# A hybrid encoder layer: block copies on GpSimd, chunk tiles in another place, stores from ScalarE's queue

## Chip, core and metric

The kernel runs on one core of a Trainium2 chip. What is measured is the device time of one execution, in microseconds (us). A core has five engines that run their own instruction streams and wait for each other by semaphores: TensorE (PE in the profile, with its weight loads as PEld), VectorE (DVE), ScalarE (ACT), GpSimd (POOL) and SyncE (SP), which here does nothing but issue DMAs. Each engine takes its instructions in order: one that waits holds all that stand behind it. DMAs are issued from an engine's queue too and then run by themselves on 16 DMA engines.

## What is computed

One layer of an encoder over 1024 tokens of width 1024, in float32: a mixer, then cross-attention into 256 memory tokens, then a SwiGLU feed-forward part. The change touches the mixer and the keys and values of the memory. The mixer has two branches, from one input projection: windowed softmax attention, and a bidirectional gated DeltaNet, whose chunks of 64 tokens each need a triangular solve and then a scan over chunks. Cut to that:

```python
def _gated_delta_chunked(q, k, v, g, beta):
    ...
    lower = jnp.where(strict, jnp.einsum('bhnid,bhnjd->bhnij', kb, k) * decay, 0.0)
    tmat = lower + jnp.eye(c, dtype=jnp.float32)
    rhs = jnp.concatenate([v * beta[..., None], kb * jnp.exp(g)[..., None]], axis=-1)
    sol = lax.linalg.triangular_solve(tmat, rhs, left_side=True, lower=True, unit_diagonal=True)
    ...
    def step(state, inp):
        qg_i, kg_i, u_i, w_i, qk_i, gl_i = inp
        v_new = u_i - jnp.einsum('bhck,bhkv->bhcv', w_i, state)
        o_i = jnp.einsum('bhck,bhkv->bhcv', qg_i, state) + jnp.einsum('bhij,bhjv->bhiv', qk_i, v_new)
        state = state * gl_i[..., None, None] + jnp.einsum('bhck,bhcv->bhkv', kg_i, v_new)
        return state, o_i
```

## The kernel before

Products that need full float32 are made of two halves: a tile is split into a high part (whi, ph, s: a cast on ScalarE, L103) and the rest (wlo, pl: a difference on VectorE, or on GpSimd where the call says so, L104), and three products take the place of one. Weights come through load_w (L119), whose loads of raw weights into wraw are issued by SyncE at L126. The scheduler of the framework puts the instructions of each engine in an order of its own from the program's order and its dependences; the orders below are what is written.

Stage 1 (ORDER_1) makes the projection of the DeltaNet's heads, the convolution, norms and decays. It ends with base_inverse (L520) for each group g of two heads: the inverses of 32x32 diagonal blocks, row by row on VectorE (L544 to L546), for all blocks at once; the last two products are V on VectorE (L548) and A on GpSimd (L549), and both are stored to d_inv in DRAM (L553). Keys turned for the scan are stored to d_kv from the tile kt (L488).

Stage 2 (ORDER_2) is a list of work: A are the attention's projections (stored to d_q and d_k), V its values, G the gates (gate_proj, L777: a Silu on ScalarE into the tile gt, L782, then a store to d_gate, L783), L the levels of a head, W two windows of attention. levels(h) (L556) builds the full inverse out of the 32x32 blocks: it loads the blocks of its head from d_inv four times (cz, cw; L564), gathers them by ten copies of a quarter or half of the partitions (m5 and c6 on ScalarE, c5 on VectorE; L573 to L577), and goes through two levels of products: pair (L598) multiplies (L603), copies the result to bs on ScalarE (L605) and multiplies again (L609); between the levels stand z5 (L614) and mov6 (L616 to L623) and behind them Z (L625, L626), stored to d_pz. window(n, g) (L632) loads its queries into qr (L643), casts them to qs on ScalarE (L645), takes the rest on GpSimd (L646), makes the scores (L654), the softmax, and the product with the values (L680, L685).

Stage 3 (ORDER_3) is the scan. M is memory_norm (L917; its transposes are at L934), s01 is one step of both groups' scans (scan, L795), W windows still open, K a block of the memory's keys (next_keys, L941: weights in_w_ckv, products pck at L949, a copy to cv on ScalarE, L951, and a store, L952) and V of its values (next_values, L954: products pcv at L965, a copy to vv, L969, and a store, L970). A step loads a chunk of d_kv and d_pz for both directions (kv and pz; L824, L825) and makes its products (L809), with copies on ScalarE (vn, L846) and VectorE. Behind the scan come the output projection and the rest of the layer.

Tiles lie in pools, and a pool that is opened where another one lay waits for the last use of what it covers. The pool tl (L743, closed with p1) holds the tiles of the levels. The pool t3 (L793), opened on the right after p1 is closed, holds the scan's tiles: those of odd steps' chunks in both groups' pz and group 0's kv, and all of group 1's kv. Even steps' pz, and group 0's even kv, lie in the pool ra. All 28 stores from the tiles kt, gt, cv and vv are issued by SyncE.

Of the kernel before, what the change touches and what calls it, by code (L numbers as in the profile page):

```python
# [10 lines left out]
F32 = mybir.dt.float32  # L11
# [8 lines left out]
P = 128  # L20
# [4 lines left out]
HALF = 512  # L25
# [9 lines left out]


ORDER_1 = ("k0 k1 E0 K0 U0 E1 K1 U1 S0 q0 v0 q1 C0 v1 E2 C1 k2 E3 k3 q2 K2 U2 v2 K3 U3 S1 q3 C2 v3 C3 B0 B1").split()
ORDER_2 = "L0 L1 A4 V A0 A1 G0 G1 L2 L3 W W W A2 A3 G2 G3 W".split()
ORDER_3 = ("M " + "s01 W K " * 5 + "s01 K " * 3 + "s01 V V").split()


# [35 lines left out]
def tile_hybrid_block(  # L77
# [6 lines left out]
    nc = tc.nc  # L84
# [396 lines left out]
    def turned_keys(h):  # L481
        g, hh = h // 2, h % 2
        for b in range(2):
            c4 = slice(4 * b, 4 * b + 4)
            pk = turned(kqv["k", h], b)
            kt = t2.tile([P, 4, P], F32, tag="kt", name="kt")
            nc.scalar.copy(kt, pk)
            nc.sync.dma_start(d_kv[g][c4, :, hh, 0].rearrange("c p n -> p c n"), kt)  # L488
            ss = squares(pk, False)
            nc.gpsimd.tensor_scalar(xk[:, h, c4], ss, EPS, None, ALU.add)  # L490
            nc.gpsimd.tensor_tensor(rootk[:, h, c4], xk[:, h, c4], phalf[:, 0:4], ALU.pow)
# [64 lines left out]
    def levels(h):  # L556

        g, hh = h // 2, h % 2

        def blocks(name):  # L560
            return tl_.tile([P, NT, 32], F32, tag=name, name=name, bufs=1)

        def fetch(dst, i, d):
            nc.sync.dma_start(dst, d_inv[g][i][d, hh].rearrange("c b r s -> (b r) c s"))  # L564

        cz = [blocks("cz0"), blocks("cz1")]
        cw = [blocks("cw0"), blocks("cw1")]
        m5, c5, c6 = blocks("m5"), blocks("c5"), blocks("c6")
        for d in range(2):
            fetch(cz[d], 1, d)  # L570
            fetch(cw[d], 0, d)
        for q in range(4):
            r = slice(32 * q, 32 * q + 32)  # L573
            nc.scalar.copy(m5[r], cz[1 - q % 2][r])
            nc.vector.tensor_copy(c5[r], cw[q % 2][r])
        for d in range(2):
            nc.scalar.copy(c6[64 * d:64 * d + 64], cw[d][64 * d:64 * d + 64])  # L577
        def part(b):
            c4 = slice(4 * b, 4 * b + 4)

            def wide(name):
                return tl_.tile([P, 4, P], F32, tag=name, name=name, bufs=2)

            L5, L6, D5, D6 = wide("L5"), wide("L6"), wide("D5"), wide("D6")
            Z = [wide("Z0"), wide("Z1")]
            for e, dst, src in ((nc.vector, D5, c5), (nc.vector, D6, c6), (nc.vector, Z[0], cz[0]), (nc.vector, Z[1], cz[1])):
                e.tensor_tensor(dst.rearrange("p c (q n) -> p c q n", q=4), bc(src[:, c4, :], 2, (P, 4, 4, 32)),
                                        bc(dmask, 1, (P, 4, 4, 32)), ALU.mult)
            Ul = wide("Ul")
            nc.sync.dma_start(Ul, d_u[g][hh, c4].rearrange("c p n -> p c n"))  # L590
            yield
            p_ = small().rearrange("p (c n) -> p c n", c=4)
            for j in range(4):
                nc.tensor.transpose(p_[:, j, :], Ul[:, j, :], ident)
            nc.vector.tensor_tensor(L5, p_, bc(cm["m5"], 1, (P, 4, P)), ALU.mult)
            nc.vector.tensor_tensor(L6, p_, bc(cm["m6"], 1, (P, 4, P)), ALU.mult)

            def pair(lt, mv, dd, w):  # L598

                yield  # L600
                p_ = small()[:, 0:4 * w].rearrange("p (c n) -> p c n", c=4)
                for c in range(4):
                    nc.tensor.matmul(p_[:, c, :], lt[:, c, :], mv[:, c, :], start=True, stop=True)  # L603
                bs = tl_.tile([P, 4, 64], F32, tag="bs", name="bs", bufs=2)[:, :, 0:w]
                nc.scalar.copy(bs, p_)  # L605
                yield
                p_ = small()[:, 0:4 * w].rearrange("p (c n) -> p c n", c=4)
                for c in range(4):
                    nc.tensor.matmul(p_[:, c, :], dd[:, c, :], bs[:, c, :], start=True, stop=True)  # L609
                return p_  # L610

            p_ = yield from pair(L5, m5[:, c4, :], D5, 32)
            z5 = tl_.tile([P, 4, 32], F32, tag="z5", name="z5", bufs=2)
            nc.scalar.mul(z5, p_, -1.0)  # L614
            nc.vector.transpose(D6[32:64, :, 0:32], z5[0:32])
            nc.vector.transpose(D6[64:96, :, 96:128], z5[96:128])  # L616
            nc.vector.tensor_copy(Z[1][32:64, :, 0:32], z5[32:64])
            nc.vector.tensor_copy(Z[0][64:96, :, 96:128], z5[64:96])
            mov6 = tl_.tile([P, 4, 64], F32, tag="mov6", name="mov6", bufs=2)
            nc.scalar.copy(mov6[0:64], Z[1][0:64, :, 0:64])  # L620
            nc.vector.tensor_copy(mov6[64:128], Z[0][64:128, :, 64:128])
            nc.scalar.copy(Z[0][0:32, :, 32:64], z5[0:32])
            nc.scalar.copy(Z[1][96:128, :, 64:96], z5[96:128])  # L623
            p_ = yield from pair(L6, mov6, D6, 64)
            nc.scalar.mul(Z[0][0:64, :, 64:128], p_[0:64], -1.0)  # L625
            nc.vector.tensor_scalar(Z[1][64:128, :, 0:64], p_[64:128], -1.0, None, ALU.mult)  # L626
            for d in range(2):
                nc.sync.dma_start(d_pz[g][d][c4, :, hh, 1].rearrange("c p n -> p c n"), Z[d])

        together([part(b) for b in range(2)])  # L630
# [109 lines left out]
    tw = p12.enter_context(pool("tw", 2))  # L740
    tw.tile([P, 384], F32, tag="sc", name="sc", bufs=8)
    vhl = tw.tile([P, NT + 1, 2, 2, 64], F32R, tag="vhl", name="vhl", bufs=1)[:, 0:NT]
    tl_ = p1.enter_context(pool("tl", 2))  # L743

    def pair():
        t = ra.tile([P, 2, HALF], F32, tag="rr", name="rr", bufs=2)
# [30 lines left out]
    def gate_proj(h):  # L777

        pp = proj(w_in[:, 2304 + h * P:2304 + (h + 1) * P])
        for hf in range(2):  # L780
            gt = trp.tile([P, HALF], F32, tag="rop", name="gt")
            nc.scalar.activation(gt, pp[hf], AF.Silu)  # L782
            nc.sync.dma_start(d_gate[h * P:(h + 1) * P, hf * HALF:(hf + 1) * HALF], gt)  # L783

    issue(ORDER_2, {"A": attn_proj, "V": value_proj, "G": gate_proj, "L": levels, "W": next_windows})
    dump("d_q", d_q); dump("d_k", d_k); dump("d_gate", d_gate)
    p1.close()
    pgs.close()
# [6 lines left out]
    def scan(g):  # L795
# [16 lines left out]
        for step in range(NT):  # L812
# [1 line left out]
            cs = (step, NT - 1 - step)  # L814

            near = step % 2 == 0
            pz = (ra.tile([P, 2, 2, 2, P], F32, tag="rr", name="pz", bufs=2) if near else tl("pz", [P, 2, 2, 2, P], bufs=1))
            if g == 0:
                kv = (ra.tile([P, 2, 2, 4, P], F32, tag="sct", name="kv") if near else tl("kv", [P, 2, 2, 4, P], bufs=1))
            else:  # L820
                kv = tl("kv", [P, 2, 2, 4, P])
            before = loaded
            for d in range(2):
                loaded = nc.sync.dma_start(kv[:, d], d_kv[g][cs[d]])  # L824
# [116 lines left out]
    def next_keys():  # L941

        ct = kv_done[0]
        kv_done[0] += 1
        whi, wlo = load_w(w_ckv[:, ct * P:(ct + 1) * P], KT, P, nc.gpsimd)
        pp = pc.tile([P, 512], F32, tag="pc", name="pck")[:, 0:ML]
        for k in range(KT):
            for i, (w, a) in enumerate(((whi, 0), (whi, 1), (wlo, 0))):
                nc.tensor.matmul(pp, w[:, k, :], mT[a][:, k, :], start=(k == 0 and i == 0), stop=(k == KT - 1 and i == 2))  # L949
        cv = mk.tile([P, 512], F32, tag="cv", name="cv", bufs=2)[:, 0:ML]  # L950
        nc.scalar.copy(cv, pp)  # L951
        nc.sync.dma_start(d_mk[ct * P:(ct + 1) * P, :], cv)  # L952

    def next_values():  # L954

        ch = kv_done[1]
        kv_done[1] += 1
        pp = [pc.tile([P, 512], F32, tag="pc", name="pcv") for _ in range(2)]
        for kp in range(4):
            whi, wlo = load_w(w_ckv[kp * 256:(kp + 1) * 256, D + ch * 512:D + (ch + 1) * 512], 2, 512)  # L960
            for t in range(2):
                for kk in range(2):
                    k = 2 * kp + kk
                    for i, (w, a) in enumerate(((whi, 0), (whi, 1), (wlo, 0))):
                        nc.tensor.matmul(pp[t], mT[a][:, k, t * P:(t + 1) * P], w[:, kk, :], start=(k == 0 and i == 0),  # L965
                                         stop=(k == KT - 1 and i == 2))
        for t in range(2):
            vv = mk.tile([P, 512], F32, tag="cv", name="vv", bufs=2)
            nc.scalar.copy(vv, pp[t])  # L969
            nc.sync.dma_start(d_mv[t, :, ch * 512:(ch + 1) * 512], vv)  # L970

    scans = [scan(g) for g in range(2)]

# [264 lines left out]
    for e in range(EARLY):  # L1238
        f = 2 * e
# [320 lines left out]
```

## Time and profile before

| what | value |
|---|---|
| time, median of 3 runs | 1537.51 us |
| lowest and highest run | 1535.87 and 1537.88 us |
| span of the profiled execution | 1537.6 us |
| busy share of PE, VectorE, ScalarE, GpSimd | 96%, 69%, 48%, 24% |

The profiled execution's own time is its span, from the first to the last instruction. In the profile a line such as `L574 ACT COPY m<-cz 32x256 ... x16 | 6.5, 404 | 8.8 <-DMA` is a group of like instructions: line of the program, engine, operation, tile written and tile read, shape, count, then busy us in all and mean ns of one, then the engine's idle us just before them and what ended it. A line of a timeline begins with the start in us from the span's start and the duration. SPq is SyncE's queue of DMA issues; a DMA's duration there is the time of its issue, and its landing comes later. A line of waits gives the engine and line that waited, what for, the us in all, how many times, and the longest. The granted clock is the share of TensorE's full speed that the chip granted in a stretch.

### The profile page before, as it was taken

What the parts mean: (1) busy time and instruction counts of PE and PEld (TensorE: products, weight loads), DVE (VectorE), ACT (ScalarE), POOL (GpSimd) and SP (SyncE); (2) the same over time, 40 slices, a digit from 0 to 9 for tenths busy, and PEclk for the clock granted to TensorE, in tenths of its full rate; (3) what the DMA queues carried; (4) which work ended last, traced back from release to release, by engine and by line L of the source; (5) the groups of instructions that cost most, each with busy time, mean ns of one, the idle gap of its engine ahead of it and who ended that gap; (6) DMA issues with size and microseconds to landing.
All of it is one profiled execution on the core that took longest, in us unless ns stands there. A gap on an engine that the chain in (4) does not pass through costs nothing. (4 is left out here: it accounts for less than half of the span.)

```text
span 1537.6 us, 21036 instructions
## 1 busy us (share of the span) xinstructions
PE 1481.4 (96%) x7451; PEld 1246.6 (81%) x7451; DVE 1067.1 (69%) x1732; ACT 743.3 (48%) x1518; POOL 374.6 (24%) x364
## 2 busy tenths in 40 slices
PE   6999999998999899999999999999999999999997
PEld 5888888787999777888888877888888888888786
DVE  6868999686788776534346387776877555696665
ACT  6578732457457665454336564323223333354532
POOL 2020210111247103253102232443433432000021
PEclk9999999999999999999999999999999999999999
DMA  6244575856997665454213354343533334853355
GB/s 207 76 116 139 156 188 155 197 173 166 309 321 219 216 208 195 138 165 136 69 55 138 104 198 130 123 130 110 171 124 96 110 104 161 291 185 96 103 176 166
DMA packets 264710, 242.95 MB, mean 158 GB/s; under 512 B 33801, under 2 KB 203678, under 8 KB 264606
## 3 DMA queue, kind: packets, MB, share of 16 engines
q1 hardware_dynamic: 264605, 241.62, 50.4%
q8 instruction: 58, 0.95, 0.3%
q14 instruction: 47, 0.38, 0.1%
HBM read 172.07 MB, written 66.88 MB: 155 GB/s over the span
## 5 line engine op out<-in xcount | busy, mean ns | idle before, releaser
L103 ACT CAST whi<-wraw 128x1024 fp32r<-128x1024 f32 x108 | 113.4, 1051 | 154.8 <-issue 31.7
L261 PE MATMUL pg<-hlo,whi 128*128 128x512 f32 x352 | 139.5, 397 | 0.0
L261 PE MATMUL pg<-hhi,whi 128*128 128x512 f32 x352 | 139.2, 396 | 0.0
L261 PE MATMUL pg<-hhi,wlo 128*128 128x512 f32 x352 | 138.5, 394 | 0.0
L104 POOL TENSOR_TENSOR wlo<-wraw,whi 128x1024 fp32r<-128x1024 f32 x38 | 91.7, 2414 | 178.7 <-ACT whi L103 169.4
L104 DVE TENSOR_TENSOR wlo<-wraw,whi 128x1024 fp32r<-128x1024 f32 x70 | 87.1, 1245 | 58.6 <-ACT whi L103 54.6
L1052 PE MATMUL pmg<-whi,b 128*128 128x512 f32 x384 | 119.0, 394 | 0.4 <-ACT b L103 0.4
L1231 PE MATMUL pA<-s,whi 128*128 128x512 f32 x352 | 109.3, 392 | 1.0 <-ACT m L1248 1.0
L1052 PEld LDWEIGHTS pmg<-whi,b 128*128 128x128 f32 x384 | 71.4, 188 | 15.3 <-ACT b L103 1.3
L1421 PE MATMUL pdX<-dhl,whi 128*128 128x512 f32 x264 | 76.1, 390 | 1.5 <-ACT dhl L103 0.8
L1231 PEld LDWEIGHTS pA<-s,whi 128*128 128x128 f32 x352 | 65.5, 188 | 14.7 <-ACT m L1248 1.5
L261 PEld LDWEIGHTS pg<-hhi,whi 128*128 128x128 f32 x352 | 66.5, 189 | 13.4 <-ACT hhi L103 0.2
L261 PEld LDWEIGHTS pg<-hhi,wlo 128*128 128x128 f32 x352 | 66.5, 189 | 12.9
L261 PEld LDWEIGHTS pg<-hlo,whi 128*128 128x128 f32 x352 | 66.4, 189 | 12.8
L1052 PE MATMUL pmg<-wlo,b 128*128 128x512 f32 x192 | 71.9, 391 | 0.0
L1308 POOL TENSOR_TENSOR act<-act,up 128x512 f32<-128x512 f32 x33 | 50.1, 1520 | 88.6 <-DVE up L1307 53.2
L103 ACT CAST whi<-araw 128x1024 fp32r<-128x1024 f32 (+1 forms) x36 | 35.4, 982 | 71.4 <-PE pdX L1421 27.6
L1231 PE MATMUL pA<-s,wlo 128*128 128x512 f32 x176 | 68.6, 391 | 0.8 <-DVE wlo L104 0.7
L104 DVE TENSOR_TENSOR wlo<-araw,whi 128x1024 fp32r<-128x1024 f32 (+1 forms) x36 | 40.8, 1133 | 38.5 <-ACT whi L103 38.4
L286 DVE SCALAR_TENSOR_TENSOR acc<-cp,cols,acc 128x1024 f32<-128x1024 f32 x48 | 62.1, 1296 | 0.1
L1280 POOL TENSOR_TENSOR sr<-wraw 128x512 f32<-128x512 f32 x22 | 30.6, 1392 | 127.0 <-DMA wraw<-in_w_gate_up_dram 125.8
L1451 POOL TENSOR_SCALAR frs<-sq 128x1 f32<-128x1 f32 x8 | 12.0, 1497 | 195.9 <-ACT jk L1440 195.0
(415 smaller groups left out, 4097.9 us busy)
## 6 DMA issues: line engine op xcount, KB each, us to landing
wraw<-in_w_gate_up_dram SPq DMA_DIRECT2D x52, 512.0 KB, 3.8
kv<-d_kv SPq DMA_DIRECT2D x32, 512.0 KB, 6.9
wraw<-in_w_in_dram SPq DMA_DIRECT2D x22, 512.0 KB, 5.6
b<-in_w_down_dram SPq DMA_DIRECT2D x20, 512.0 KB, 7.0
araw<-d_as SPq DMA_DIRECT2D x20, 512.0 KB, 3.9
pz<-d_pz SPq DMA_DIRECT2D x32, 256.0 KB, 5.3
wraw<-in_w_ckv_dram SPq DMA_DIRECT2D x16, 512.0 KB, 8.7
wraw<-in_w_out_dram SPq DMA_DIRECT2D x16, 512.0 KB, 4.0
```

The lines of the kernel that those rows point to most:

```text
L103: nc.scalar.copy(hi, src)
L104: (eng or nc.vector).tensor_tensor(lo, src, f32(hi), ALU.subtract)
L261: nc.tensor.matmul(p_, w[:, k, :], ah[a][:, k, :], start=(k == 0 and i == 0), stop=(k == nk - 1 and i == 2))
L286: nc.vector.scalar_tensor_tensor(acc, cp[:, t:t + S], taps[t], acc, ALU.mult, ALU.add)
L1052: nc.tensor.matmul(pp[t], act[a][:, k, tt], w_[:, kk, :], start=(k == 0 and i == 0), stop=(k == KT - 1 and i == 2))
L1231: nc.tensor.matmul(out_, w[a][:, k, :], xx[b_][:, k, :], start=(start and k == 0 and i == 0), stop=(k == HK - 1 and i == 2), skip_group_ch ...
L1280: nc.gpsimd.tensor_tensor(s[0], b_[:, 0:HK], b_[:, HK:], ALU.add)
L1308: nc.gpsimd.tensor_tensor(o_, o_, up, ALU.mult)
L1421: nc.tensor.matmul(banks[t], a[:, k - k0, tt], w, start=(first and k == 0 and i == 0), stop=(k == NB - 1 and i == 2), skip_group_check=not ...
L1451: nc.gpsimd.tensor_scalar(rs, sq[:, 1, t:t + 1], sq[:, 0, t:t + 1], D * EPS, ALU.add, ALU.add)
```

## The change

Three things are changed, and no arithmetic. The ten copies in levels move to GpSimd. A new entry T behind L3 in ORDER_2 calls scan_chunks, which closes the levels' pool (now on its own stack ptl) and opens a pool tk in its place; the odd steps' pz of both groups, group 0's odd kv and group 1's kv lie there and not in t3. The stores from kt (8), gt (8), cv (8) and vv (4) are issued from ScalarE's queue. Lines below the change are shifted: by 8 from L745, by 9 from about L830.

```diff
--- before.py
+++ after.py
@@ -35,7 +35,7 @@
 
 
 ORDER_1 = ("k0 k1 E0 K0 U0 E1 K1 U1 S0 q0 v0 q1 C0 v1 E2 C1 k2 E3 k3 q2 K2 U2 v2 K3 U3 S1 q3 C2 v3 C3 B0 B1").split()
-ORDER_2 = "L0 L1 A4 V A0 A1 G0 G1 L2 L3 W W W A2 A3 G2 G3 W".split()
+ORDER_2 = "L0 L1 A4 V A0 A1 G0 G1 L2 L3 T W W W A2 A3 G2 G3 W".split()
 ORDER_3 = ("M " + "s01 W K " * 5 + "s01 K " * 3 + "s01 V V").split()
 
 
@@ -485,7 +485,7 @@
             pk = turned(kqv["k", h], b)
             kt = t2.tile([P, 4, P], F32, tag="kt", name="kt")
             nc.scalar.copy(kt, pk)
-            nc.sync.dma_start(d_kv[g][c4, :, hh, 0].rearrange("c p n -> p c n"), kt)
+            nc.scalar.dma_start(d_kv[g][c4, :, hh, 0].rearrange("c p n -> p c n"), kt)
             ss = squares(pk, False)
             nc.gpsimd.tensor_scalar(xk[:, h, c4], ss, EPS, None, ALU.add)
             nc.gpsimd.tensor_tensor(rootk[:, h, c4], xk[:, h, c4], phalf[:, 0:4], ALU.pow)
@@ -571,10 +571,10 @@
             fetch(cw[d], 0, d)
         for q in range(4):
             r = slice(32 * q, 32 * q + 32)
-            nc.scalar.copy(m5[r], cz[1 - q % 2][r])
-            nc.vector.tensor_copy(c5[r], cw[q % 2][r])
+            nc.gpsimd.tensor_copy(m5[r], cz[1 - q % 2][r])
+            nc.gpsimd.tensor_copy(c5[r], cw[q % 2][r])
         for d in range(2):
-            nc.scalar.copy(c6[64 * d:64 * d + 64], cw[d][64 * d:64 * d + 64])
+            nc.gpsimd.tensor_copy(c6[64 * d:64 * d + 64], cw[d][64 * d:64 * d + 64])
         def part(b):
             c4 = slice(4 * b, 4 * b + 4)
 
@@ -740,7 +740,15 @@
     tw = p12.enter_context(pool("tw", 2))
     tw.tile([P, 384], F32, tag="sc", name="sc", bufs=8)
     vhl = tw.tile([P, NT + 1, 2, 2, 64], F32R, tag="vhl", name="vhl", bufs=1)[:, 0:NT]
-    tl_ = p1.enter_context(pool("tl", 2))
+    ptl = ExitStack()
+    tl_ = ptl.enter_context(pool("tl", 2))
+    tk = []
+
+    def scan_chunks():
+
+        ptl.close()
+        tk.append(p12.enter_context(pool("tk", 2)))
+
 
     def pair():
         t = ra.tile([P, 2, HALF], F32, tag="rr", name="rr", bufs=2)
@@ -780,9 +788,9 @@
         for hf in range(2):
             gt = trp.tile([P, HALF], F32, tag="rop", name="gt")
             nc.scalar.activation(gt, pp[hf], AF.Silu)
-            nc.sync.dma_start(d_gate[h * P:(h + 1) * P, hf * HALF:(hf + 1) * HALF], gt)
-
-    issue(ORDER_2, {"A": attn_proj, "V": value_proj, "G": gate_proj, "L": levels, "W": next_windows})
+            nc.scalar.dma_start(d_gate[h * P:(h + 1) * P, hf * HALF:(hf + 1) * HALF], gt)
+
+    issue(ORDER_2, {"A": attn_proj, "V": value_proj, "G": gate_proj, "L": levels, "W": next_windows, "T": scan_chunks})
     dump("d_q", d_q); dump("d_k", d_k); dump("d_gate", d_gate)
     p1.close()
     pgs.close()
@@ -814,11 +822,12 @@
             cs = (step, NT - 1 - step)
 
             near = step % 2 == 0
-            pz = (ra.tile([P, 2, 2, 2, P], F32, tag="rr", name="pz", bufs=2) if near else tl("pz", [P, 2, 2, 2, P], bufs=1))
-            if g == 0:
-                kv = (ra.tile([P, 2, 2, 4, P], F32, tag="sct", name="kv") if near else tl("kv", [P, 2, 2, 4, P], bufs=1))
+            pz = (ra.tile([P, 2, 2, 2, P], F32, tag="rr", name="pz", bufs=2) if near else
+                  tk[0].tile([P, 2, 2, 2, P], F32, tag=f"pz{g}", name="pz", bufs=1))
+            if g == 0 and near:
+                kv = ra.tile([P, 2, 2, 4, P], F32, tag="sct", name="kv")
             else:
-                kv = tl("kv", [P, 2, 2, 4, P])
+                kv = tk[0].tile([P, 2, 2, 4, P], F32, tag=f"kv{g}", name="kv", bufs=1 + g)
             before = loaded
             for d in range(2):
                 loaded = nc.sync.dma_start(kv[:, d], d_kv[g][cs[d]])
@@ -949,7 +958,7 @@
                 nc.tensor.matmul(pp, w[:, k, :], mT[a][:, k, :], start=(k == 0 and i == 0), stop=(k == KT - 1 and i == 2))
         cv = mk.tile([P, 512], F32, tag="cv", name="cv", bufs=2)[:, 0:ML]
         nc.scalar.copy(cv, pp)
-        nc.sync.dma_start(d_mk[ct * P:(ct + 1) * P, :], cv)
+        nc.scalar.dma_start(d_mk[ct * P:(ct + 1) * P, :], cv)
 
     def next_values():
 
@@ -967,7 +976,7 @@
         for t in range(2):
             vv = mk.tile([P, 512], F32, tag="cv", name="vv", bufs=2)
             nc.scalar.copy(vv, pp[t])
-            nc.sync.dma_start(d_mv[t, :, ch * 512:(ch + 1) * 512], vv)
+            nc.scalar.dma_start(d_mv[t, :, ch * 512:(ch + 1) * 512], vv)
 
     scans = [scan(g) for g in range(2)]
```

## Prediction

> **What bounds the kernel now.** I read the busy times first, then the chain of waits, then TensorE's (PE's) waits and the stretches in which it idles, and last the timelines of the queues around those stretches.
>
> ```profile
> span 1537.6 us, 21036 instructions
> ...
> PE 1481.4 (96%) x7451; PEld 1246.6 (81%) x7451; DVE 1067.1 (69%) x1732; ACT 743.3 (48%) x1518; POOL 374.6 (24%) x364
> ...
> PE 39%; DVE 1%; DMA 1%; ACT 0%; SPq 0%; issue 0%; POOL 0%; DVEq 0%; POOLq 0%; ACTq 0%
> ```
>
> PE is busy for 1481.4 of 1537.6 us, and the chain that ended last is almost all PE. So the change can only win where PE stands still, or where its clock is lowered: some 56 us in all. By the instruction orders of the two programs, PE's instructions are the same in number, and their order differs only from about 100 to 555 us. What PE waits for there, and its stretches (columns: start and end, length, busy us of PE, PEld, DVE, ACT, POOL, granted clock, DMA share, GB/s):
>
> ```profile
> PE pck L949 <- ACT whi L103: 3.5, 1, 3.5
> PE ps L609 <- ACT bs L605: 3.4, 1, 3.4
> PE pcv L965 <- ACT whi L103: 2.9, 2, 1.6
> PE psc L809 <- ACT vn L846: 2.0, 1, 2.0
> ```
>
> ```profile
> 283.00:293.00 10.00, 6.58 (x25) 5.70 (x24) 4.96 (x12) 3.75 (x9) 1.52 (x1) 0.66 1.07 242
> 386.00:396.00 10.00, 9.32 (x54) 9.13 (x55) 4.40 (x13) 3.32 (x6) 2.48 (x2) 0.70 1.07 326
> 400.00:440.00 40.00, 39.90 (x330) 38.97 (x330) 36.80 (x107) 18.94 (x42) 11.73 (x8) 1.00 1.00 304
> 500.00:530.00 30.00, 26.80 (x170) 23.60 (x170) 23.41 (x49) 19.91 (x54) 6.25 (x11) 1.00 0.53 166
> 530.00:550.00 20.00, 15.05 (x69) 11.07 (x68) 15.45 (x29) 12.97 (x23) 0.20 (x1) 1.00 0.92 342
> ```
>
> Two stalls are far above the rest, 3.4 and 3.5 us, and after these two alone the granted clock falls: 0.66 over the ten us from 283, 0.70 over the ten from 386. The stretch 500 to 530 holds stalls of up to 2.0 us, and its clock stays at 1.00. So each large stall costs twice: 3.4 + (1 - 0.66) x 10 = 6.8 us, and 3.5 + (1 - 0.70) x 10 = 6.5 us. A stall cut to 2 us costs 2 us.
>
> **Levels' copies on POOL.** The first stall, on ScalarE and PE:
>
> ```profile
> 281.62 0.82 ACT L574 COPY m<-cz 32x256 f32<-32x256 f32 x2 [2.76 <-DMA cz<-d_inv]
> 283.07 0.41 ACT L577 COPY c<-cw 64x256 f32<-64x256 f32 x1 [0.64 <-DMA cw<-d_inv]
> 283.74 0.40 ACT L577 COPY c<-cw 64x256 f32<-64x256 f32 x1 [0.26 <-DMA cw<-d_inv]
> 284.16 0.60 ACT L782 ACTIVATE gt<-pg 128x512 f32<-128x512 f32 x1
> 284.78 0.81 ACT L574 COPY m<-cz 32x256 f32<-32x256 f32 x2
> 285.78 0.62 ACT L645 CAST qs<-qr 128x512 fp32r<-128x512 f32 x1 [0.18 <-DMA qr<-d_q]
> 286.31 0.64 ACT L605 COPY bs<-ps 128x256 f32<-128x256 f32 x2
> ```
>
> The copy into bs, which PE waits for, stands in ScalarE's order behind six block copies of a later head, and these wait for loads of the base inverse that have hardly been issued. PE is not late because of the work of the copies, but because they wait at the head of the queue. In the changed order none of them is on ScalarE. But one waiting instruction stays: the cast of qs (L645) now stands before the last two steps of that level, and its load is the next thing behind the loads of the inverse:
>
> ```profile
> 281.93 1.44 SPq L643 DMA_DIRECT2D qr<-d_q  x2
> ```
>
> The cast began at 285.78, released by this load, so the load landed just before that. Before that step PE has, by the changed order, sixteen more products of the projection, and these follow each other every 0.23 us:
>
> ```profile
> 282.67 0.40 PE L261 MATMUL pg<-hlo,whi 128*128 128x512 f32 x1
> 282.91 0.40 PE L261 MATMUL pg<-hhi,wlo 128*128 128x512 f32 x1
> ```
>
> So it asks for the step some 3.6 us later, at about 287 instead of 283.3. Behind qs ScalarE has a gate activation, its store, z, two small copies and mov, about 2.5 us by the rows above: ready at about 289, a stall of 2 us if nothing else moves. Bounds: nothing left (-6.8), if the loads come earlier; both the stall and a longer clock drop (+3), if they come 3 us later. I take 2 us left without a clock drop: -4.8.
>
> What the copies cost where they go is not in the trace; POOL copies no such block here. Nearest rows:
>
> ```profile
> L574 ACT COPY m<-cz 32x256 f32<-32x256 f32 x16 | 6.5, 404 | 8.8 <-DMA cz<-d_inv 8.7
> L575 DVE COPY c<-cw 32x256 f32<-32x256 f32 x16 | 4.6, 284 | 10.0 <-DMA cw<-d_inv 9.8
> L577 ACT COPY c<-cw 64x256 f32<-64x256 f32 x8 | 3.2, 404 | 7.5 <-DMA cw<-d_inv 7.0 <-ACT gt L782 0.3
> L886 POOL TENSOR_TENSOR ol<-ol,of 128x256 f32<-128x256 f32 x12 | 8.6, 739 | 8.6 <-DVE ol L870 8.1 <-DVE es L668 0.5
> L886 DVE TENSOR_TENSOR ol<-ol,of 128x256 f32<-128x256 f32 x4 | 1.5, 418 | 0.0
> ```
>
> The same 128x256 sum takes POOL 739 ns and VectorE 418, 1.77 times as long. At that ratio a copy costs 284 x 1.77 = 0.50 us; bounds 0.28 (as VectorE) and 0.74 (as the sum). Ten of a head run in a row on POOL: 5 us, where ScalarE and VectorE shared 6 x 0.404 = 2.4 and 4 x 0.284 = 1.1 us side by side. VectorE is rid of 4.6 us in all, ScalarE of 9.7. POOL has room:
>
> ```profile
> 269.60 0.16 POOL L547 MEMSET A<- 128x32 f32 x1 [54.47 <-DVE A L546]
> 272.62 2.74 POOL L549 TENSOR_TENSOR A<-A,bB 128x1024 f32<-128x1024 f32 x1 [2.86 <-DVE V L548]
> 274.26 1.18 DVE L617 COPY Z<-z 32x128 f32<-32x128 f32 x1
> 275.47 0.22 DVE L618 COPY Z<-z 32x128 f32<-32x128 f32 x1
> ```
>
> It idles 54.47 us in front of the last step of the second base inverse, and that idle time hides the copies of heads 0 and 1. What it does not hide is VectorE: that engine is the one which works through the base inverse in those 54 us, and the copy at 274.26 took 1.18 us where its twin took 0.22; it ended as POOL's product ended (272.62 + 2.74 = 275.36). So VectorE can stand still while POOL works. If no copy meets it, the inverse ends 8 x 0.284 = 2.3 us earlier; if each of the 20 copies stops it for its whole 0.50 us, 10 - 2.3 = 7.7 us later. I take +1.5 us for this and for the changed order of PE between the stalls (bounds -1 and +5).
>
> The Trainium skill ("SBUF — State Buffer", section "Who interferes with whom") states that GpSimd shares a port pair with VectorE as an exclusive lock, so that whoever starts second blocks until the first has finished. By that rule, the trace agrees with 1.18 against 0.22 us, and the copies would delay the inverse (rival three).
>
> **Scans' chunk tiles.** The second stall, with SyncE's queue and ScalarE, and the landing times of the weight loads between 340 and 460 us:
>
> ```profile
> 369.02 0.33 SPq L783 DMA_DIRECT2D d_gate<-gt  x1
> 369.45 1.33 SPq L824 DMA_DIRECT2D kv<-d_kv  x3
> ...
> 373.00 0.54 SPq L126 DMA_DIRECT2D wraw<-in_w_ckv_dram  x1
> ...
> 385.58 1.04 ACT L103 CAST whi<-wraw 128x1024 fp32r<-128x1024 f32 x1 [1.79 <-DMA wraw<-in_w_ckv_dram]
> ```
>
> ```profile
> DMA to landing us min/median/max: 7.5/8.7/12.6
> ```
>
> PE waits for the first w_ckv weights. Their load was issued at 373.00 and landed after 12.6 us, the longest of eight; the median is 8.7. Right ahead of it SyncE issued the chunk loads of the odd steps and of group 1, all at once: their tiles lie where the gate's store at 369.02 had to be done first. With the pool in the place of the levels' tiles they are released by the levels' last products:
>
> ```profile
> L609 PE MATMUL ps<-bs,D x128: 190/276/473, 235.3 to 358.2; 128*128 128x32 f32 x64, 128*128 128x64 f32 x64
> ```
>
> The last begins at 358.2 (its times are min, median and max in ns, then first and last start), so the burst can leave some 15 us ahead of the weight load instead of 4. The weight load itself is released by the last transposes of the memory tiles, as before. At the median landing it comes 12.6 - 8.7 = 3.9 us earlier, more than the stall of 3.5. Bounds: all of it (-6.5), and nothing (0), if the burst still meets the load. I take half a us left and no clock drop: -6.0.
>
> What is late next is the end of the stretch, 530 to 550, where PE idles 20 - 15.05 = 4.95 us, mostly for weight casts. In the changed order SyncE issues the residual's loads and gpost behind the first big store of d_mix, so behind the w_ckv loads, not among them: up to 4 us to gain, and as they then meet the output projection's weights up to 3 us to lose. I take -1.
>
> **Stores on ScalarE's queue.** 28 stores move. The one at 369.02 took the issuing queue 0.33 us, so 28 x 0.33 = 9.2 us of ScalarE, about what the copies gave back (9.7). SyncE loses that and the waits in front of these stores:
>
> ```profile
> SPq L952 <- ACT cv L951: 6.7, 3, 3.6
> ```
>
> On ScalarE these vanish, since it wrote the tile itself; SyncE's loads behind them (L126, L824) are issued up to 3.6 us earlier. New is that a store's other waits now hold ScalarE. In the changed order several stores also wait for the landing of a DMA issued some places earlier:
>
> ```profile
> kv<-d_kv SPq DMA_DIRECT2D x32, 512.0 KB, 6.9
> ```
>
> Behind gate stores that is an earlier gate store, mostly over by then, behind two of the cv stores a chunk load of 6.9 us. Queued behind a blocked store are the casts ph and whi and the copy vn, for which PE waits within 2 us already (rows above). Bounds: 0, if each landing is past, and +12, if two blocks grow into stalls with a clock drop. I take +2.
>
> **The sum.** -4.8 + 1.5 - 6.0 - 1 + 2 = -8.3 us. The profiled span, 1537.6, equals the median of 1537.51; so 1529.3 us.
>
> **The rivals.**
>
> One: only the second stall goes. qs, waiting for its load in front of the level's last steps, keeps the first stall over 3 us. For it speaks that the load sits behind all inverse loads in SyncE's queue; against it, 3.6 us more PE work. Then -6.0 - 1 + 2 + 1.5 = -3.5: 1534 us.
>
> Two, slower: ScalarE's queue is held by its stores' waits between 390 and 520, where the DMA share is 1.00 (400 to 440). It decides once a block outlasts about 3.5 us, since PE then idles as long as in the two known stalls. Three such blocks (two cv stores, one vv store) cost 3 x 6.5 = 19.5 us against 11.8 won: 1545 us. Against it, PE lost only 0.1 us in 400 to 440 while SyncE waited there, and ScalarE is busy for half of that time only.
>
> Three: POOL's copies stop VectorE in the second base inverse. At the full 7.7 us the loads of the inverse and of qr come that much later, at 293.5, and the level's end at about 296.5 against 287: a stall of 9.5 and a drop of 3.4, 12.9 us for the old 6.8. With the rest (-6.0 - 1 + 2) that is 1538.7 us. Against it, POOL's copies need 10 us of 54. The Trainium skill's rule, named above, gives this result if every copy meets a VectorE instruction that needs the pair.
>
> Four: all goes, and SyncE's freer queue takes away half of the smaller stalls too (3.2 us in 500 to 530, 4.95 in 530 to 550): -11.8 - 4 = 1522 us.
>
> **How the numbers follow.** The forecast gets 0.44, with a range of its own from 1525 to 1534; rival one 0.16, two 0.18, three 0.12, four 0.10. The time predicted is that of the first, 1529.3. The range from 1521 to 1543 leaves out the far half of rival two and some of four. This kernel's measurement can tell about 0.2% (3 us) from no change. Faster than 1534.4: the forecast nearly whole, four, and half of one, with a little of three: 0.64. Slower than 1540.6: most of two and a third of three, and something for what I have not seen: 0.22. Between them 0.14.
>
> **What would show it.** The wait of L609's product for bs at 283 gone or under 2 us, and a granted clock of 1.00 there; no wait of pck over 1 us at the first w_ckv weights, whose load lands in under 9 us; chunk loads issued well ahead of the last gate store. POOL's block copies at 0.3 to 0.7 us. Wrong would be: a wait of PE for a product of ScalarE over 3 us anywhere from 390 to 550 with ScalarE idle behind a store; VectorE's inverse ending later than 272.5; or stalls of the old size in new places.

## The result, and the profile after

The changed kernel takes 1551.34 us (median of 4 runs, 1547.21 to 1553.09) where the kernel before took 1536.69: a ratio of 1.0085, 95% interval 1.0071 to 1.0099. It is slower by 13 us. The forecast was 8 us faster, and the time lies above the whole range.

The page of the changed kernel (its profiled execution's span is 1551.4 us):

```profile
span 1551.4 us, 21026 instructions
...
PE 1491.8 (96%) x7451; PEld 1255.9 (81%) x7451; DVE 1064.8 (69%) x1716; ACT 732.8 (47%) x1494; POOL 392.4 (25%) x404
```

PE runs the same 7451 instructions as before but is busy 1491.8 - 1481.4 = 10.4 us longer. So most of the loss is no waiting: PE works, at a lower clock. PE's waits between 100 and 600 us (total, times, longest):

```profile
PE pow L685 <- ACT ph L103: 7.4, 5, 2.7
PE pmg L1061 <- ACT whi L103: 5.8, 2, 5.0
PE psc L817 <- DVE kv L846: 2.5, 1, 2.5
PE ps L603 <- DVE mov L621: 2.2, 2, 2.1
PE psc L817 <- ACT vn L855: 1.8, 1, 1.8
```

Of the two large waits of before, pck at 383 is gone from this list, and the level's step at 283 is down from 3.4 to 2.1 us (L603 for mov). The other four lines are new or larger. Stretches of 50 us, first of the kernel before, then of the changed one (start and end, length, busy us of PE, PEld, DVE, ACT, POOL, granted clock, DMA share, GB/s):

```profile
250.00:300.00 50.00, 46.01 (x238) 39.13 (x238) 38.36 (x80) 16.92 (x37) 5.72 (x4) 0.93 0.77 195
300.00:350.00 50.00, 49.49 (x283) 42.59 (x282) 41.40 (x101) 29.03 (x72) 6.41 (x6) 1.00 0.61 171
350.00:400.00 50.00, 43.06 (x275) 38.06 (x274) 29.73 (x78) 31.66 (x70) 9.16 (x11) 0.93 0.80 227
400.00:450.00 50.00, 47.96 (x396) 46.67 (x396) 43.30 (x127) 24.29 (x56) 17.23 (x11) 1.00 1.01 311
500.00:550.00 50.00, 41.86 (x238) 34.66 (x238) 38.86 (x77) 32.88 (x76) 6.45 (x12) 1.00 0.68 237
550.00:600.00 50.00, 49.13 (x228) 40.22 (x228) 30.67 (x42) 27.56 (x43) 0.20 (x1) 1.00 0.50 167
```

```profile
250.00:300.00 50.00, 47.59 (x245) 40.38 (x245) 35.32 (x71) 14.74 (x31) 12.83 (x21) 0.93 0.74 191
300.00:350.00 50.00, 48.26 (x263) 41.74 (x262) 40.01 (x96) 24.49 (x62) 6.40 (x10) 0.93 0.56 160
350.00:400.00 50.00, 44.91 (x272) 38.55 (x271) 33.98 (x89) 33.76 (x75) 9.09 (x11) 0.93 0.70 221
400.00:450.00 50.00, 45.34 (x341) 43.69 (x341) 38.16 (x109) 23.85 (x58) 14.77 (x10) 0.93 0.87 266
500.00:550.00 50.00, 44.80 (x286) 40.06 (x284) 40.80 (x95) 33.16 (x92) 13.64 (x22) 0.97 0.51 161
550.00:600.00 50.00, 43.08 (x175) 34.16 (x175) 27.06 (x26) 24.19 (x32) 0.00 (x0) 0.93 0.70 245
```

From each row follow two losses: PE's idle time (50 less its busy time) and the clock's (50 times what is missing to 1.00; a hundredth is half a us). After less before, in us:

| stretch | idle | clock | together | forecast put there |
|---|---|---|---|---|
| 250 to 300 | -1.6 | 0 | -1.6 | -4.8 |
| 300 to 350 | +1.2 | +3.5 | +4.7 | (in +1.5) |
| 350 to 400 | -1.9 | 0 | -1.9 | -6.0 |
| 400 to 450 | +2.6 | +3.5 | +6.1 | +2 |
| 500 to 550 | -2.9 | +1.5 | -1.4 | (in -1) |
| 550 to 600 | +6.0 | +3.5 | +9.5 | (in -1) |

With the stretches not shown, idle time from 100 to 600 goes from 26.0 to 28.5 us and the clock's loss from 7.0 to 19.0: 14.5 us more, against 13.8 in the spans. Five sixths of it is clock.

### The profile page after: what moved, and what is told of

The parts are those of the page before. It is cut to its first block, busy times and chain, and to the rows that moved or that the text cites. A ratio compares the mean times of both kernels' runs of the same rounds, so it can differ in the third digit from the quotient of the medians.

```text
span 1551.4 us, 21026 instructions
## 1 busy us (share of the span) xinstructions
PE 1491.8 (96%) x7451; PEld 1255.9 (81%) x7451; DVE 1064.8 (69%) x1716; ACT 732.8 (47%) x1494; POOL 392.4 (25%) x404
## 5 line engine op out<-in xcount | busy, mean ns | idle before, releaser
L261 PE MATMUL pg<-hlo,whi 128*128 128x512 f32 x352 | 140.0, 398 | 0.0
L261 PE MATMUL pg<-hhi,whi 128*128 128x512 f32 x352 | 139.6, 397 | 0.2 <-ACT hhi L103 0.2
L261 PE MATMUL pg<-hhi,wlo 128*128 128x512 f32 x352 | 139.1, 396 | 0.0
L261 PEld LDWEIGHTS pg<-hhi,whi 128*128 128x128 f32 x352 | 66.6, 190 | 13.9 <-ACT hhi L103 0.5
L261 PEld LDWEIGHTS pg<-hhi,wlo 128*128 128x128 f32 x352 | 66.9, 190 | 13.0
L261 PEld LDWEIGHTS pg<-hlo,whi 128*128 128x128 f32 x352 | 66.9, 190 | 12.8
```

The lines of the kernel that those rows point to most:

```text
L261: nc.tensor.matmul(p_, w[:, k, :], ah[a][:, k, :], start=(k == 0 and i == 0), stop=(k == nk - 1 and i == 2))
```

## The experiments

All ratios are to the kernel before, run beside it on the same chip, with 95% intervals. "Idle" and "clock" are the two losses between 100 and 600 us, from the profile of that kernel.

| kernel | ratio | interval | idle, clock |
|---|---|---|---|
| copies alone | 0.9973 | 0.9956 to 0.9991 | 21.6, 5.0 |
| chunk tiles alone | 1.0033 | 1.0021 to 1.0045 | 25.5, 10.0 |
| stores alone | 0.9997 | 0.9982 to 1.0011 | 21.4, 7.0 |
| changed, without stores | 0.9996 | 0.9982 to 1.0010 | 22.6, 9.5 |
| changed, without chunk tiles | 1.0040 | 1.0021 to 1.0059 | 28.6, 16.5 |
| changed, without copies | 1.0065 | 1.0041 to 1.0089 | 27.8, 11.5 |
| changed, again | 1.0078 | 1.0048 to 1.0107 | 29.3, 17.0 |
| changed, cv stores back | 1.0069 | 1.0046 to 1.0092 | 26.0, 14.0 |
| changed, vv stores back | 1.0073 | 1.0043 to 1.0103 | 27.7, 15.0 |
| changed, cv and vv back | 1.0048 | 1.0029 to 1.0067 | 25.7, 12.0 |
| changed, gate stores back | 0.9986 | 0.9972 to 0.9999 | 21.9, 5.0 |
| changed, six gate stores back | 1.0047 | 1.0030 to 1.0065 | 28.2, 12.0 |
| changed, last two gate stores back | 1.0001 | 0.9989 to 1.0013 | 23.8, 8.5 |
| changed, vr off ScalarE | 1.0091 | 1.0076 to 1.0106 | 29.3, 18.5 |
| changed, xr behind weights | 1.0032 | 1.0017 to 1.0047 | 27.5, 10.0 |

### The three parts, alone and two by two

The copies alone: the three lines of levels from the diff.

> The kernel before with the ten block copies of levels on GpSimd and nothing else. If the copies do what the prediction said (ScalarE no longer blocked at 283), the stall of 3.4 us at 283 shrinks to 2 us or less and the time falls by 3 to 7 us, to 1530 to 1534. If the copies are what cost the time (VectorE held up in the second base inverse, or the cast of qs taking the place of the copies as the blocker), it is 1538 to 1545, with the loads of d_inv later than 277.

Faster, 0.9973, which is 4.2 us and inside the 3 to 7 expected. PE's stall in the level is 1.7 us (for mov), and no clock is lost after it. It has the lowest ratio of this study, though its interval and that of the changed kernel with its gate stores back (0.9986) overlap: the version to take is the copies alone. PE's wait for the first weights of pck was under 0.6 us here too, without the chunk tiles: the wait of 3.5 us went with the order.

The chunk tiles alone: the pool, T, and the tiles of pz and kv.

> The kernel before with the pool tk for the scans' chunks and nothing else. If the pool does what the prediction said, the wait of pck for the first w_ckv weights (3.5 us at 383) falls under 1 us and the time falls by 4 to 7 us. If the new order of PE, with its many small stalls and a lower clock after each, comes from this part, the time is 1542 to 1552, with clock losses after stalls of 1 to 3 us between 340 and 600, and a late cast of values in the output projection (5 us near 592).

Slower, 1.0033. pck waits no longer, but a stall of 2.5 us stands near 379, and in every kernel that has the chunk tiles one of that size stands between 370 and 380 (2.45 to 2.48 us in all thirteen profiles). In the changed kernel, ScalarE and then PE:

```profile
373.56 1.28 ACT L663 ACT_TABLE_LOAD   x1
...
377.27 0.56 ACT L103 CAST ph<-ptw 128x512 fp32r<-128x512 f32 x1
```

```profile
377.88 0.80 PE L685 MATMUL pow<-ph,vhl 128*128 128x512 f32 x1 [2.46 <-ACT ph L103]
```

The load of a table and four exponentials of the softmax (L663) fill ScalarE from 373.56 to 377.27, and the cast of ph comes behind them. In the kernel before it is the same run of work, and PE has gate projections (L261) beside it to the end (in the changed kernel the last of these begins at 368.4, before the run does):

```profile
360.00 1.28 ACT L663 ACT_TABLE_LOAD   x1
```

```profile
363.48 0.39 PE L261 MATMUL pg<-hhi,wlo 128*128 128x512 f32 x1
```

What the changed kernel pays there, stall and clock (0.72), shows in its ten us from 373:

```profile
373.00:383.00 10.00, 6.53 (x24) 4.45 (x24) 6.24 (x14) 7.46 (x17) 3.06 (x6) 0.72 1.05 396
```

So the cover that hid this run went to an earlier place when the tiles gave the scheduler other dependences.

The stores alone: the four lines with dma_start.

> The kernel before with the 28 stores on ScalarE's queue and nothing else. If the stores are what cost the time (ScalarE held by a store that waits for the landing of a chunk load, as the 4.1 us at 422 in the changed kernel), it is 1543 to 1550, with ScalarE idle for 2 to 4 us in front of stores of cv or vv. If they are free (rest of the engine covers them), 1535 to 1538, and SyncE's waits for cv and gt are gone.

No difference, 0.9997, though one block did occur: ScalarE stood 3.8 us in front of a cast of ph, released by a landing, and PE 2.8 us for it. What that cost was won elsewhere in its profile (idle 21.4 us against 26.0); the wait of pck was gone here as well.

Then two parts at a time:

> The changed kernel with its 28 stores back on SyncE's queue. If the stores cost the time, this is 1528 to 1534, faster than before. If the order that came with the chunk tiles costs it, this is 1543 to 1552, near the changed kernel.

> The changed kernel with the scans' chunks back in the pool t3. Alone, the copies gave 0.9973 and the stores 0.9997. If the two add, this is 0.995 to 0.999, some 1531 to 1537. If the stores are harmful wherever the copies have changed the order, it is over 1.002.

> The changed kernel with the block copies back on ScalarE and VectorE. Alone, the chunks gave 1.0033 and the stores 0.9997. If the chunk tiles together with the stores are what costs the time (a store of cv or vv on ScalarE waits for the landing of chunk loads that the new pool lets out in its way), this is 1.006 to 1.013. If parts only add, it is 1.001 to 1.005, and the rest of the changed kernel's 1.0085 comes from copies and stores together.

> The changed kernel once more on the same chip as the parts: 1.007 to 1.010 if its verdict holds; its stalls at 342, 378, 424, 550 and 592 us come again at the same instructions if they are the program's order, and at others if they are chance.

Without the stores the kernel is as fast as before, which neither of its two expectations had; without the chunk tiles it is over the 1.002 named for stores that harm in the copies' order, and without the copies it is in the range named for chunk tiles and stores together. The parts do not add. Alone they make -0.27, +0.33 and -0.03%, together +0.85%. The stores cost nothing alone, but 0.67% on top of the copies (0.9973 to 1.0040) and 0.9% on top of the other two (0.9996 to 1.0085). No part carries the loss alone. The changed kernel, run again, showed the stalls near 376, 422, 547 and 590 at the same instructions (2.5, 3.6, 2.9 and 5.5 us), so they belong to the program. The one at 342 did not: it came as two of 0.7 and 1.0 us.

### Which stores

The stores of cv back on SyncE's queue; PE's order is that of the changed kernel, instruction for instruction:

```diff
-        nc.scalar.dma_start(d_mk[ct * P:(ct + 1) * P, :], cv)
+        nc.sync.dma_start(d_mk[ct * P:(ct + 1) * P, :], cv)
```

> The changed kernel with the eight stores of cv back on SyncE's queue; the order of every instruction on PE is that of the changed kernel. If ScalarE, held at a cv store by the landing of a chunk load (4.1 and 5.2 us at 420 in the two profiles of the changed kernel), is a main cost, the stall of 2.5 to 3.6 us of L817 for kv at 422 is gone with the lower clock behind it: 4 to 7 us less, a ratio to before of 1.003 to 1.006. If the block only moves idle time of ScalarE, it stays at 1.007 to 1.010.

The block is real. In the changed kernel a store of cv waits on ScalarE's queue for the landing of a chunk load, and the queue behind it waits too:

```profile
417.82 0.37 ACT L960 COPY cv<-pck 128x256 f32<-128x256 f32 x1 [3.02 <-PE pck L958]
421.89 0.33 ACTq L961 DMA_DIRECT2D d_mk<-cv  x1
422.31 0.58 ACT L688 COPY ao<-pow 64x512 f32<-64x512 f32 x1 [4.12 <-DMA kv<-d_kv]
```

```profile
423.93 1.00 PE L817 MATMUL psc<-kv,pz 128*128 128x128 f32 x6 [2.53 <-DVE kv L846]
```

cv was ready at 418.2; its store went out at 421.9, and the copy of ao that VectorE and then PE waited for at 422.3. With the stores back the stall at 422 is gone, and between 400 and 450 the losses fall from 4.7 + 3.5 to 2.3 + 0. But the time, 1.0069, cannot be told from the changed kernel's by its interval: less than expected.

The stores of vv back (40 lines of PE's order differ):

> The changed kernel with the four stores of vv back on SyncE's queue; 40 lines of PE's order differ, all behind 540 us. If these stores cause the stall of 5.0 to 5.5 us in the output projection at 590 (the residual's loads and mvr issued some 10 us later than where the stores are SyncE's), it is gone: 6 to 9 us less, 1.002 to 1.005. If that stall comes from the chunk tiles alone, it stays, and so does the time, 1.007 to 1.010.

1.0073; the stall near 590 stayed (5.3 us), so these stores are not its cause. Both back:

> Both: the changed kernel with cv and vv stores on SyncE's queue, kt and gt stores on ScalarE's. If these two causes are all of the cost of the stores, 0.998 to 1.002, as with all stores back (0.9996). If the gate's stores cost too, 1.003 to 1.006.

1.0048, in the interval named for "the gate's stores cost too". So the two together are worth some 0.37% by the first measurement of the changed kernel (1.0085) and 0.30% by the second (1.0078), whose interval overlaps this one. And the gate's stores back, cv and vv on ScalarE:

> The changed kernel with the eight gate stores back on SyncE's queue. If cv and vv are the causes, this stays at 1.006 to 1.010. If the gate's stores are a cause (ScalarE held between the levels' steps, VectorE's wait for a late store of Z at 340), it falls to 1.001 to 1.005.

0.9986. With eight stores of 28 back the loss is gone while cv and vv are still on ScalarE, so the idea that cv and vv are the causes falls, as far as it says that they are enough. PE's order is another one there, from 368 us on (over 800 of its instructions stand in another place), and the stall near 590 is gone. So the next question is whether the stores cost, or the order that comes with them. The last gate's stores decide the order alone, which gives two kernels that cross the two:

```diff
-            nc.scalar.dma_start(d_gate[h * P:(h + 1) * P, hf * HALF:(hf + 1) * HALF], gt)
+            (nc.scalar if h == 3 else nc.sync).dma_start(d_gate[h * P:(h + 1) * P, hf * HALF:(hf + 1) * HALF], gt)
```

> The changed kernel with the gate stores of heads 0 to 2 (six of eight) back on SyncE's queue; PE's order is that of the changed kernel, instruction for instruction. If the order that the scheduler built is what costs, this stays at 1.005 to 1.010 with the stall of 5 us at 587 to 592. If it is the stores themselves on ScalarE's queue, most of their cost goes with six of eight: 0.999 to 1.003.

and, with nc.sync and nc.scalar exchanged in that line, the last two:

> The changed kernel with the gate stores of head 3 alone (two of eight) back on SyncE's queue; PE's order is, instruction for instruction, that of the kernel with all eight back, which gave 0.9986; 26 of 28 stores stay on ScalarE. If the order is what costs, 0.997 to 1.001 and no stall at 587. If the stores are, 1.004 to 1.009.

With the changed kernel's PE order and six stores fewer on ScalarE: 1.0047. With the other order and two stores fewer: 1.0001. So the two stores of head 3 are worth 0.84%, and most likely by the order: in the changed kernel they take 2 x 0.33 us of ScalarE themselves, at 365.72 and 369.41, each within 0.1 us of the end of the Silu that wrote its tile. No kernel has these two stores in one place and the order of the other, so this is argued, not shown. The six others are worth 0.38% in an order that stays as it is (1.0085 to 1.0047; 0.31% from the second measurement, 1.0078, whose interval overlaps), and 0.15% in the other (0.9986 to 1.0001, whose intervals overlap): that is the measured cost of stores on ScalarE's queue. The expectation of 1.005 to 1.010 for the six stores was just missed, since it left the stores no cost of their own.

### What in that order costs: the stall near 590

Each kernel with the chunk tiles and the last gate stores on ScalarE has a stall of 3.5 to 5.5 us in the output projection (after, and the ones without copies, with cv, vv or six gates back). SyncE's queue in the changed kernel, then ScalarE and PE:

```profile
571.49 0.47 SPq L1035 DMA_DIRECT2D gpost<-in_g_mix_post_dram  x1
572.00 2.28 SPq L1071 DMA_DIRECT2D xr<-in_x_dram  x4
575.55 0.38 SPq L1117 DMA_DIRECT2D mvr<-d_mv  x1
577.96 19.02 SPq L126 DMA_DIRECT2D wraw<-in_w_out_dram  x4
```

```profile
588.30 1.90 ACT L103 CAST vr<-mvr 128x2048 fp32r<-128x2048 f32 x1 [2.95 <-DMA mvr<-d_mv]
...
591.25 1.04 ACT L103 CAST whi<-wraw 128x1024 fp32r<-128x1024 f32 x1
```

```profile
592.35 1.09 PE L1061 MATMUL pmg<-whi,s 128*128 128x512 f32 x2 [5.00 <-ACT whi L103]
```

The first reading was that ScalarE's queue is blocked by the cast of vr, which waits for its load and then runs 1.9 us ahead of the weights' cast. The edit takes it off ScalarE:

```diff
-        split(*hl, raw)
+        split(*hl, raw) if hl is kr_ else (nc.gpsimd.tensor_copy(hl[0], raw), nc.gpsimd.tensor_tensor(hl[1], raw, f32(hl[0]), ALU.subtract))
```

> The changed kernel with both halves of vr (the memory's values for cross-attention) made on GpSimd, so that ScalarE does not cast them; SyncE's order is the same, PE's differs in 7 lines. If the stall of 5 us at 590 comes from ScalarE's queue, held by the vr cast that waits for mvr (2.9 us) and then runs 1.9 us in front of the weights' casts, the stall falls under 1 us with the lower clock behind it: 5 to 9 us less, 1.002 to 1.005. If the weights of the output projection are late, it stays at 4 to 5 us, 1.006 to 1.010.

It fell: 1.0091, and a stall of 3.5 us stays, now with ScalarE waiting for the weights themselves. Its ScalarE, GpSimd and VectorE:

```profile
587.49 1.04 ACT L103 CAST whi<-wraw 128x1024 fp32r<-128x1024 f32 x1 [2.56 <-DMA wraw<-in_w_out_dram]
```

```profile
588.31 4.56 POOL L1118 TENSOR_TENSOR vr<-mvr,vr 128x2048 fp32r<-128x2048 f32 x1
```

```profile
588.56 5.39 DVE L104 TENSOR_TENSOR wlo<-wraw,whi 128x1024 fp32r<-128x1024 f32 x1 [2.92 <-ACT whi L103]
```

That wlo took 5.39 us where it takes 1.2 otherwise, which made a second stall of 2.5 us: the new place of vr brought its own cost. What stayed is that the weights landed at 587.5, behind four loads of xr (2 MB) and mvr (1 MB) that were issued just ahead of them. So those loads go behind two further loads of weights:

```diff
-                nc.sync.dma_start(raw, src.rearrange("(k p) n -> p k n", p=P))
+                w_loads.append(nc.sync.dma_start(raw, src.rearrange("(k p) n -> p k n", p=P)))
...
-            nc.sync.dma_start(xr, res[tok, :])
+            with (tc.issue_after(w_loads[-3].ins) if res is x and hf == 0 else ExitStack()): nc.sync.dma_start(xr, res[tok, :])
```

> The changed kernel with the four loads of the residual (xr, 2 MB) for the output projection held behind two further loads of its weights on SyncE's queue; mvr comes ahead of them by that, and PE's order differs in 5 lines. If the stall of 3.5 to 5.5 us near 590 is the burst of xr in front of those weights, it falls under 1 us: 5 to 8 us less, 1.002 to 1.005. If not, it stays at 1.007 to 1.010.

1.0032, and the stall of 5 us is gone. Its queue, and the stretch from 550 to 600 of this kernel and of the one with all gate stores back:

```profile
576.08 4.33 SPq L126 DMA_DIRECT2D wraw<-in_w_out_dram  x2
580.47 2.30 SPq L1071 DMA_DIRECT2D xr<-in_x_dram  x4
```

```profile
550.00:600.00 50.00, 48.09 (x209) 38.75 (x208) 27.14 (x26) 23.45 (x31) 0.00 (x0) 0.98 0.75 257
```

```profile
550.00:600.00 50.00, 50.00 (x226) 41.38 (x225) 29.22 (x29) 26.62 (x39) 3.37 (x6) 1.00 0.69 238
```

Idle and clock there are 1.9 + 1.0 us, against 6.9 + 3.5 in the changed kernel. So the burst is worth some 0.5% of the 0.85%: the largest piece that was taken away with the rest of the order kept, and it is an effect of the order in which the loads were issued.

## Why the prediction was wrong, point by point

**The sum against the runs.** -8.3 us was forecast, +13.8 measured in the profiles. One part of the gain was there: -4.8 from the copies is -4.2 by the run of copies alone (0.27% of 1537). The other, -6.0 from the chunk tiles, was not: alone they cost 0.33%, 5 us. The steps, one by one:

**"A stall cut to 2 us costs 2 us."** This is the step that cost most. It came from one profile in which stalls up to 2.0 us had kept the clock at 1.00. In the changed kernel a stall of 1.6 us drew a lower clock, and 2.05 us at 288 did as well. First ten us around a stall of 1.95 and one of 1.96 us in the kernel before, then the drops behind the stalls of 2.05, 1.59 and 1.85 us in the changed one:

```profile
444.00:454.00 10.00, 8.05 (x64) 7.61 (x63) 7.28 (x25) 6.66 (x18) 3.84 (x3) 1.00 0.97 293
504.00:514.00 10.00, 8.04 (x63) 7.71 (x63) 7.41 (x17) 8.55 (x31) 1.86 (x5) 1.00 0.19 54
```

```profile
288.74:295.57 6.83, 6.83 (x25) 6.04 (x25) 3.52 (x9) 1.16 (x3) 3.33 (x4) 0.50 0.86 229
343.35:350.18 6.83, 6.83 (x26) 6.05 (x26) 5.08 (x17) 3.12 (x7) 0.00 (x0) 0.50 0.00 0
408.20:411.61 3.41, 3.41 (x18) 3.31 (x17) 2.29 (x6) 3.28 (x10) 1.92 (x2) 0.50 0.33 87
```

A drop here is to 0.50 and lasts 3.41 or 6.83 us, so it costs 1.7 or 3.4 us, and a stall of 1.6 to 2.1 us may cost itself or that much more; the same stall at 288 drew no drop in the kernel with the copies alone (1.7 us). Its length does not settle it. The changed kernel has eight drops, three long and five short, 18.8 us (19.0 in the table's rounding), where the two of the kernel before cost 6.8. Of the 18.8, 10.2 us came behind stalls of at most 2.05 us, and 8.5 behind four of 2.46 to 5.00, for which the sum had no drop either. Which stalls draw one is in part luck: in the second profile of the changed kernel the level's stall was 1.06 us and drew none.

All 17 profiles show more of it. Within each, all changes of the granted clock lie whole multiples of 3.413 us apart, to 3 ns. If the time from 100 to 600 us is cut at these steps, the clock was halved behind each of the 56 pieces at full clock in which PE was busy, by its records, for under 45%, behind 16 of 30 at 45 to 55%, and behind 3 of 2240 at 70% or more. So it is the busy share of such a piece that counts for the most part, and a stall of 2 us counts less if a step cuts it in two, as the one of 1.96 us at 504 was (at 504.70). The Trainium skill ("TensorE: Matmul & The Clock Gate", Part 1) states that the clock is set by activity in a window of about 3.4 us that runs freely, so that the phase counts. The traces agree, with 3.413 us; its rule that idle gaps over some 3.4 us are the danger, taken as a threshold, is not what these rows show.

**The first stall.** The mechanism was right, and the size was partly luck: qs held ScalarE until its load landed, and the level's end came late by 2.05 us, where 2 were forecast. But 1.3 of them are two products that VectorE had in front of its half of mov (L621), which the forecast did not name. ScalarE and VectorE in the changed kernel, then VectorE's last product of the second base inverse:

```profile
283.31 0.62 ACT L645 CAST qs<-qr 128x512 fp32r<-128x512 f32 x1 [6.04 <-DMA qr<-d_q]
286.27 1.30 DVE L587 TENSOR_TENSOR D<-c,dmask 128x512 f32<-128x512 f32 x2
```

```profile
268.43 2.10 DVE L548 TENSOR_TENSOR V<-A,bB 128x1024 f32<-128x1024 f32 x1
```

The groups of the copies on GpSimd:

```profile
L575 POOL COPY c<-cw 32x256 f32<-32x256 f32 x16 | 8.6, 540 | 11.0 <-DVE D L587 10.3
L574 POOL COPY m<-cz 32x256 f32<-32x256 f32 x16 | 7.6, 474 | 19.1 <-PE ps L603 7.2 <-PE ps L609 6.4 <-DMA cz<-d_inv 4.9
L577 POOL COPY c<-cw 64x256 f32<-64x256 f32 x8 | 3.6, 448 | 5.5 <-DVE D L587 5.1
```

They took 0.45 to 0.54 us each where 0.50 was worked out. The second base inverse did not end later: its last product ended at 270.5, and the prediction had named 272.5 as the bound. So rival three did not come at its price: 20 of the copies ran among the rows of that inverse, between 219 and 239 us, and VectorE's 120 row products of both inverses (L544, L546) took 40.7 us in all where they had taken 39.5, so some 1.2 us against the 7.7 of the bound.

**The second stall.** The landing times of the weight loads between 340 and 460 us (min, median, max), the first of them and the cast that waited for it, in the changed kernel:

```profile
DMA to landing us min/median/max: 4.4/5.4/5.8
```

```profile
387.86 0.56 SPq L126 DMA_DIRECT2D wraw<-in_w_ckv_dram  x1
...
393.69 1.05 ACT L103 CAST whi<-wraw 128x1024 fp32r<-128x1024 f32 x1 [0.34 <-DMA wraw<-in_w_ckv_dram]
```

So a load landed sooner behind its issue than the 12.6 us of before, but not earlier: the prediction had it issued "as before", at 373.00, and it was issued at 387.86, and landed some 8 us later than before. PE did not wait for it because other work stood in front of pck, which began at 395.0. The runs of the copies alone and of the stores alone, which leave the tiles where they were, have no such wait of pck either. And -6.0 became -1.9, since the cover of another run of ScalarE's work was moved away: 2.46 us with a clock drop that no row of the kernel before could show. The prediction's "+1.5 us for this and for the changed order of PE", bounds -1 and +5, was the term for that. It was mis-sized by far: the order, at the chunk tiles (0.33% alone, where -6.0 us were forecast) and at the last gate stores together, is by these runs the larger part of the loss.

**The end of the stretch.** "I take -1", with "up to 3 us to lose" where the residual's loads meet the output projection's weights. The collision was named rightly, and its size was wrong: 5.0 us and a clock drop, about 7 us by the run that takes it away (0.46% from 1.0078 to 1.0032).

**The stores.** Rival two's mechanism occurred as described, a cv store waiting for a chunk load with the copies behind it: 4.1 us at 422, 5.2 in the second profile, 6.4 in the kernel without chunk tiles, where PE stood 3.6 us. "I take +2" against 0.38% or 6 us for six gate stores in one order and 0.15% in the other. But rival two said 1545 us by that mechanism alone; the cv stores put back gave no difference that can be told, and cv and vv together some 0.3 to 0.4%.

What stays open is the stretch from 300 to 350, +4.7 us in the profile. VectorE there waited for a store of Z to land, and PE for VectorE:

```profile
340.73 0.69 DVE L587 TENSOR_TENSOR Z<-cz,dmask 128x512 f32<-128x512 f32 x1 [3.35 <-DMA d_pz<-Z]
```

```profile
342.76 1.36 PE L603 MATMUL ps<-m,L 128*128 128x32 f32 x8 [1.59 <-DVE L L596]
```

PE stood 2.8 us there in the kernel without chunk tiles, and a microsecond or less in the others. No run took that store's wait away by itself. How much of the 1.0085 is the two gate stores' order apart from the burst (1.0032 with the burst gone against 1.0001) was not taken further either.

## What to carry to other kernels

Where a scheduler orders the instructions, an edit of one DMA's queue can change the order of hundreds of instructions behind it, and that may cost more than the edit itself; compare orders first, and cross the order of one kernel with the edit of the other before blaming the edit. A bound engine at 96% can lose more by several short stalls than by two long ones, once each may draw a lower clock: count the stalls, not only their sum. A store on a computing engine's queue can wait there for the landing of another transfer, and holds all that is behind it.

## What the runs showed of the hardware

TensorE's granted clock was 1.00 or 0.50 in the 17 profiles, its changes lay whole multiples of 3.413 us apart, and a drop behind a stall lasted 3.41 us, two or at most three times that. A stall of 1.59 us was followed by a drop of 6.83 us, while two of 1.95 and 1.96 us were followed by none. A difference on VectorE of 128x1024 took 5.39 us while GpSimd ran one of 128x2048 for 4.56 us from 0.25 us earlier, against 1.26 us in the mean of the changed kernel; that agrees with what the prediction cited from the Trainium skill ("SBUF — State Buffer", section "Who interferes with whom"): whoever starts second waits for the whole of the first.
